# Modulation rows: three of eight weight tiles of the second half on VectorE instead of TensorE

## The chip, the core and the metric

The kernel runs on one core of one Trainium2 chip. The metric is the device time of one execution in microseconds (us). TensorE is called PE in the profile, VectorE DVE, ScalarE ACT, GpSimd POOL and SyncE SP; SP's queue issues nearly all the DMAs.

## What is computed

The reference is one layer of a diffusion backbone: 1024 latent tokens and 256 context tokens of width 1024, all in float32. What matters here is its beginning. Two vectors (the condition c and the learned vector of the context) go through silu and a 1024 x 6144 weight matrix; the first 2048 columns give the shift and the scale that modulate the normed tokens ahead of the first projection:

```python
mod = jax.nn.silu(c) @ w_mod[l] + b_mod[l]
mod_c = jax.nn.silu(c_ctx)[None, :] @ w_mod[l] + b_mod[l]
sh1, sc1, g1, sh2, sc2, g2 = jnp.split(mod, 6, axis=-1)
sh1c, sc1c, g1c, sh2c, sc2c, g2c = jnp.split(mod_c, 6, axis=-1)
h = modulate(rms_norm(x, norm1_w[l]), sh1, sc1)
hc = modulate(rms_norm(ctx, norm1_w[l]), sh1c, sc1c)
aq, ak, av, mq, mk, mv, mo, mg, ga, gm = split_in_proj(h @ w_in[l])
aqc, akc, avc, mqc, mkc, mvc, moc, mgc, gac, gmc = split_in_proj(hc @ w_in[l])
```

Behind it come windowed attention, a bidirectional mLSTM, a gated merge and a convolutional feed-forward part.

## The kernel before

`layer_kernel` runs the stages one after the other: `attention_setup` and `stage_startup` (the change is in the latter), then attention, mLSTM, the merges and the feed-forward tail. A matrix product of accuracy float32 is done with operands split into a high and a low part (`split_from`: ACT copies the high part, line 44; DVE subtracts it, line 49) and three matmuls (`mm3`, lines 90 to 92).

`stage_startup` works in this order:

- Lines 303 to 312: the small vectors are loaded and turned, and `sil` gets silu of both condition vectors: for each k one column pair, 128 x 2.
- Lines 373 to 380, the modulation rows: two halves i = 0 and 1, each with eight weight tiles of 128 x 1024 (512 KB, line 376). Each tile is the moving operand of two f32 matmuls, 512 columns each, with the 128 x 2 block `sil[:, k]` as weights; they accumulate in `pm[i]`, two rows for the two condition vectors. The tiles come from `block`, a ring of 11 buffers that is shared with the context tiles `x0` and `x1`, the later x tiles and the weights that follow. So a load waits until the tile 11 places ahead of it in the ring has been used.
- Lines 335 to 347, `modulation(i)`: the two rows are copied out of PSUM into `mrow` (half on DVE, half on ACT), turned by eight small transposes (`pmT`, line 341), and made into four columns of `mods` (bias and scale for latent and context tokens) by six DVE operations on 128 x 4.
- Lines 323 to 328, `norm`: squares and their sum on ACT (`xj`), the root on POOL, the scaling of the token tile on DVE (line 328).
- Lines 349 to 371: the normed context is turned on PE (`turn_context`, tiles `xct`), modulated and split on ACT and DVE (`hfc`, `hcH`, `hcL`). Blocks 0 and 1 need the first half of the modulation, blocks 2 and 3 the second.
- Lines 389 to 447: the weights for the context keys and values are loaded (line 70) and split, and the products `pkc` and `pvc` follow.
- Lines 396 to 407 and 448 to 468, `k_stack` and `context_keys`: the normed keys are doubled into the two tiles `kk` and `kl` of 128 x 512, turned, and stored.
- Lines 471 to 503: the context's mLSTM projections `cx`, with the turning and modulating of the latent tokens (`xt`, `hf`, `hH`, `hL`) between them.

PSUM: `bank` hands out eight banks by number; `tp_tile` takes banks 3, 4 and 5 in turn, `mm_tile` 0 and 1.

In this stage the order of instructions on each engine is set when the program is built, by a scheduler that goes by the order of the text, by dependencies and by its own model of times; on the chip each engine keeps to the order it was given. In attention the order on PE, DVE, ACT and POOL is pinned by hand (class `Pinned`; all pinned instructions show line 516).

The later modulation rows have another form already (`mod_product` and `mod_row`, lines 217 to 249): DVE multiplies each weight tile of 128 x 512 by the column of `sil` and adds (`macc`), and four matmuls with a 128 x 128 block of `macc` as weights and one column of `expo` (filled with -0.5) as the moving operand sum over the partitions; the factor -2 restores the sum.

Of the kernel before, what the change touches and what calls it, by code (L numbers as in the profile page):

```python
# [8 lines left out]
F32 = mybir.dt.float32  # L9
F32R = mybir.dt.float32r  # L10
AF = mybir.ActivationFunctionType
ALU = mybir.AluOpType
# [4 lines left out]
P = 128  # L17
D = 1024
# [3 lines left out]
KT = D // P  # L22
# [20 lines left out]
def copy_act(nc, out, in_, scale=1.0):  # L43
    nc.scalar.activation(out, in_, AF.Copy, scale=scale)  # L44
# [55 lines left out]
def layer_kernel(ctx: ExitStack, tc: tile.TileContext, A: dict, out: bass.AP, dbg=None):  # L100
# [71 lines left out]
    with ExitStack() as st:  # L172
        at = attention_setup(E, st)
        stage_startup(E, at)
        if "hT" in dbg:
            for k in range(KT):
                nc.sync.dma_start(dbg["hT"][0, k * P : (k + 1) * P], hH[k].bitcast(F32))
                nc.sync.dma_start(dbg["hT"][1, k * P : (k + 1) * P], hL[k].bitcast(F32))
        if dbg.get("stop") != "hT":
            stage_attention(E, st, at)  # L180
# [109 lines left out]

def stage_startup(E, at):
    nc, tc, A, ident, expo, vecT, mods = E.nc, E.tc, E.A, E.ident, E.expo, E.vecT, E.mods
    mm_tile, tp_tile, s_tile, wts = E.mm_tile, E.tp_tile, E.s_tile, E.wts
    H = KT // 2
    with ExitStack() as st:
        sp = st.enter_context(tc.tile_pool(name="st1", bufs=1, reuse_waits="tile"))
        wp = st.enter_context(tc.tile_pool(name="stw", bufs=2, reuse_waits="tile"))
        xp = st.enter_context(tc.tile_pool(name="stx", bufs=11, reuse_waits="tile"))

        def block(name):  # L300
            return xp.tile([P, D], F32, tag="x", name=name)
# [7 lines left out]
        sil = E.sil3  # L309
# [7 lines left out]
        def load(i):  # L317
            t = block(f"x{i}")
            src = A["ctx"][i * P : (i + 1) * P] if i < NCB else A["x"][(i - NCB) * P : (i - NCB + 1) * P]
            nc.sync.dma_start(t, src)  # L320
            return t

        def norm(i, t):
            junk = wp.tile([P, D], F32, tag="junk", name=f"xj{i}", bufs=1)
            nc.scalar.activation(junk, t, AF.Square, accum_out=ss[:, i : i + 1])
            nc.gpsimd.tensor_scalar(ss[:, i : i + 1], ss[:, i : i + 1], 1.0 / D, EPS, op0=ALU.mult, op1=ALU.add)
            nc.gpsimd.tensor_tensor(rs[:, i : i + 1], ss[:, i : i + 1], expo[:, 0:1], op=ALU.pow)
            nc.vector.tensor_scalar(t, t, rs[:, i : i + 1], None, op0=ALU.mult)
# [3 lines left out]
        pm = [[pm0[:2, 0:512], pm0[:2, 512:1024]], [mm_tile("pm2")[:2], mm_tile("pm3")[:2]]]  # L332
        bT = vecT[:, 32:48].rearrange("p (s k) -> p s k", s=2)

        def modulation(i):
            mrow = sp.tile([P, 1024], F32, name=f"mrow{i}", tag="mrow")[:2]
            nc.vector.tensor_copy(mrow[:, 0:512], pm[i][0])
            copy_act(nc, mrow[:, 512:1024], pm[i][1])
            pT = tp_tile(f"pmT{i}")
            for j in range(8):  # L340
                nc.tensor.transpose(pT[:, 2 * j : 2 * j + 2], mrow[:, j * P : (j + 1) * P], ident[:2, :2])
            pTv = pT[:, :16].rearrange("p (s k c) -> p s c k", s=2, c=2)
            ks = slice(H * i, H * i + H)
            for c in (1, 0):
                nc.vector.tensor_tensor(mods[:, 2 + c, ks], pTv[:, 0, c], bT[:, 0, ks], op=ALU.add)
                nc.vector.scalar_tensor_tensor(mods[:, c, ks], pTv[:, 1, c], 1.0, bT[:, 1, ks], op0=ALU.add, op1=ALU.add)
                nc.vector.tensor_tensor(mods[:, c, ks], mods[:, c, ks], vecT[:, 16 + H * i : 16 + H * i + H], op=ALU.mult)

        def modulated(c, k, hi, lo, src, nm):
            w = hi.shape[1]  # L350
            f = sp.tile([P, 512], F32, tag="hf", name=f"hf{nm}", bufs=3)[:, :w]
            nc.scalar.activation(f, src, AF.Identity, bias=mods[:, 2 + c, k : k + 1], scale=mods[:, c, k : k + 1])
            split_from(nc, hi, lo, f)
# [4 lines left out]
        def turn_context(k2):  # L358
            pt = tp_tile(f"xct{k2}")
            for j in range(2):  # L360
                for c in range(NCB):
                    k = 2 * k2 + j
                    nc.tensor.transpose(
                        pt[:, (2 * j + c) * P : (2 * j + c + 1) * P], xc[c][:, k * P : (k + 1) * P], ident
                    )
            return pt

        def context(k2, pt):
            for j in range(2):
                k = 2 * k2 + j  # L370
                modulated(1, k, *hc[k], pt[:, j * NCTX : (j + 1) * NCTX], f"c{k}")

        for i in range(2):
            for k in range(KT):
                w = block(f"wm{i}_{k}")
                nc.sync.dma_start(w, A["w_modA"][i][:, k])
                for n in range(2):
                    nc.tensor.matmul(
                        pm[i][n], sil[:, k], w[:, n * 512 : (n + 1) * 512], start=k == 0, stop=k == KT - 1
                    )  # L380
                if i == 0 and k in (3, 4):
                    xc.append(load(k - 3))
            if i == 0:
                modulation(0)
                for c in range(NCB):
                    norm(c, xc[c])
                for k2 in range(2):
                    context(k2, turn_context(k2))
        at.constants()
        wkc = wts.load(A["w_kc"], 256, block)  # L390
        pts = [turn_context(k2) for k2 in (2, 3)]
        modulation(1)
        for k2 in (2, 3):
            context(k2, pts[k2 - 2])

        def k_stack(kf, nh, name):
            w = nh * HD
            kk = wp.tile([P, 512], F32, tag="kk", name=f"kk{name}", bufs=1)
            kh = kk[:, : 2 * w].rearrange("p (h r d) -> p h r d", r=2, d=HD)
            kv = kf.rearrange("p (h d) -> p h d", d=HD)  # L400
            for r in range(2):
                copy_act(nc, kh[:, :, r].bitcast(F32R), kv)
            kl = wp.tile([P, 512], F32, tag="kl", name=f"kl{name}", bufs=1)
            kl4 = kl[:, : 2 * w].rearrange("p (h r d) -> p h r d", r=2, d=HD)
            for r in range(2):
                nc.vector.tensor_tensor(kl4[:, :, r].bitcast(F32R), kv, kh[:, :, r], op=ALU.subtract)
            return kk, kl
# [40 lines left out]
        def context_keys():  # L448
            for c in range(NCB):
                ps = pkc[c]  # L450
                sq = wp.tile([P, 256], F32, tag="sq", name=f"sqc{c}", bufs=1)
                nc.scalar.activation(sq, ps[:, :256], AF.Square)
                rstd = wp.tile([P, 4], F32, tag="ssc", name=f"ssc{c}", bufs=2)
                nc.vector.tensor_reduce(rstd, sq.rearrange("p (h d) -> p h d", d=HD), axis=AX.X, op=ALU.add)
                nc.gpsimd.tensor_scalar(rstd, rstd, 1.0 / HD, EPS, op0=ALU.mult, op1=ALU.add)
                nc.gpsimd.tensor_tensor(rstd, rstd, expo[:, :4], op=ALU.pow)
                kf = wp.tile([P, 256], F32, tag="qf", name=f"kcf{c}", bufs=2)
                kv4 = kf.rearrange("p (h d) -> p h d", d=HD)
                nc.vector.tensor_tensor(
                    kv4, ps[:, :256].rearrange("p (h d) -> p h d", d=HD), rstd[:, :, None].to_broadcast([P, NKV, HD]), op=ALU.mult  # L460
                )
                nc.vector.tensor_tensor(kv4, kv4, at.qw[:, 1, None, :].to_broadcast([P, NKV, HD]), op=ALU.mult)
                kk, kl = k_stack(kf, NKV, f"c{c}")
                for src, dst in ((kk, at.KcA), (kl, at.KcB)):
                    pt = tp_tile(f"kct{c}")
                    for h in range(NKV):
                        nc.tensor.transpose(pt[:, h * P : (h + 1) * P], src[:, h * P : (h + 1) * P], ident)
                    copy_act(nc, dst[:, :, c * P : (c + 1) * P], pt.rearrange("p (h t) -> p h t", h=NKV))
# [3 lines left out]
        for i in range(4):  # L472
# [5 lines left out]
            w = []  # L478
# [2082 lines left out]
```

## Time and profile before

| | |
|---|---|
| three runs, median | 1935.49 us |
| lowest and highest | 1934.72 and 1941.44 us |
| the profiled execution | 1934.33 us |
| its span, first to last instruction | 1932.5 us |
| its mean granted TensorE clock | 0.996 |
| DVE, ACT, POOL busy | 1348.9, 971.5, 344.5 us |
| HBM read and written | 201.67 and 74.00 MB |

A row of the timeline has start, length, engine, line, operation, output tile <- inputs, sizes and the count of like instructions; in brackets the idle time of the engine before it and what ended it. A group row has the count, the busy time and mean ns of one, and behind the bar the idle time before them. A row on a tile gives shortest, median and longest duration in ns. PEld is the weight load of PE, which overlaps the matmuls. Matmuls are pipelined, so the duration of one is longer than the step from one to the next. "issue" is time in which an engine waited for nothing that the profile shows. In the table by stage the clock is a share of full speed.

### The profile page before, as it was taken

To read this page: it belongs to the slowest core of one execution; us is meant where nothing else is said; L and a number is where in the kernel's file an instruction comes from. 1 tells how busy PE (TensorE), PEld (TensorE's weight loads), DVE (VectorE), ACT (ScalarE), POOL (GpSimd) and SP (SyncE) were. 2 spreads that over 40 slices of the span, in tenths; PEclk is the share of its full clock that TensorE was granted. 3 is DMA by queue.
4 is the path that set the end of the run, shared out by engine and by line. 5 is a ranking of instruction groups with operands and counts; after the bars stand their busy time and mean duration, and the time that the engine had idled before them with its cause. 6 is when DMAs were issued, how large, how long until landed. Compare 5 with 4: busy or idle time off the path is not lost.

```text
span 1932.5 us, 28336 instructions
## 1 busy us (share of the span) xinstructions
PE 1904.1 (99%) x10108; PEld 1648.8 (85%) x10108; DVE 1348.9 (70%) x2611; ACT 971.5 (50%) x1872; POOL 344.5 (18%) x594
## 2 busy tenths in 40 slices
PE   8999999999999999999999999999999999999999
PEld 3988888888888899999998788887888888888887
DVE  2877767767776456576676458359988888895564
ACT  4855556556556354646444323257545454464441
POOL 1323333333332132434231000010000000000000
PEclk9999999999999999999999999999999999999999
DMA  8733223223223321513145778312555544499741
GB/s 313 226 98 83 83 70 99 63 80 93 72 74 82 93 73 36 127 47 98 42 129 172 250 234 285 128 66 77 185 200 181 196 153 179 148 332 329 253 165 44
DMA packets 133246, 273.33 MB, mean 141 GB/s; under 512 B 14433, under 2 KB 46833, under 8 KB 129777
## 3 DMA queue, kind: packets, MB, share of 16 engines
q1 hardware_dynamic: 132336, 267.33, 41.8%
q0 software_dynamic: 768, 4.20, 1.4%
q8 instruction: 79, 1.29, 0.3%
q14 instruction: 63, 0.51, 0.1%
HBM read 201.67 MB, written 74.00 MB: 143 GB/s over the span
## 4 chain that ended last, share of the span: by engine, by line
PE 92%; DVE 4%; DMA 2%; ACT 1%; issue 1%; POOL 0%; SPq 0%; DVEq 0%; ACTq 0%; POOLq 0%
PE g L516 9%; PE kv L516 7%; PE pq L516 6%; PE mo L516 5%; PE op L516 5%; PE pa L2169 4%; PE pa L2167 4%; PE pa L2168 4%; PE s L516 4%; PE ya L516 4%; PE po L516 4%; PE pt L516 3%; PE ym L516 3%; PE q L516 2%; PE dx L2167 2%; PE dx L2168 2%
## 5 line engine op out<-in xcount | busy, mean ns | idle before, releaser
L516 DVE CUSTOM_DVE_ANT_0 P<-s,maskA,nsink 128x640 f32<-128x640 f32 (+1 forms) x112 | 103.4, 923 | 81.6 <-PE s L516 80.0
L516 ACT ACTIVATE P<-P,st 128x640 f32<-128x640 f32 (+1 forms) x128 | 102.4, 800 | 88.8 <-DVE st L516 88.7
L516 ACT ACTIVATE ph<-pt 128x512 fp32r<-128x512 f32 x152 | 90.3, 597 | 63.9 <-PE pt L516 62.3
L516 DVE TENSOR_TENSOR pl<-pt,ph 128x512 fp32r<-128x512 f32 x152 | 101.0, 680 | 25.9 <-ACT ph L516 25.7
L516 POOL TENSOR_SCALAR P<-P,st 128x640 f32<-128x640 f32 (+1 forms) x128 | 110.5, 881 | 32.0 <-ACT ph L516 10.9
L516 PE MATMUL g<-hH,fh 128*128 128x512 f32 x256 | 106.8, 417 | 0.2 <-ACT fo L516 0.2
L516 PE MATMUL g<-hH,fl 128*128 128x512 f32 x256 | 101.1, 395 | 0.0
L516 PE MATMUL g<-hL,fh 128*128 128x512 f32 x256 | 101.0, 395 | 0.0
L516 PE MATMUL pt<-ident,P 128*128 128x128 f32 x608 | 91.3, 273 | 3.8 <-DVE pl L516 3.8
L516 PEld LDWEIGHTS pt<-ident,P 128*128 128x128 f32 x608 | 75.7, 141 | 15.5 <-issue 3.9
L516 PE MATMUL pq<-w1h,hH 128*128 128x384 f32 (+1 forms) x256 | 87.1, 340 | 0.0
L516 PE MATMUL kv<-w1h,hH 128*128 128x384 f32 x256 | 86.9, 340 | 0.0
L516 PE MATMUL pq<-w1l,hH 128*128 128x384 f32 (+1 forms) x256 | 86.9, 340 | 0.0
L516 PE MATMUL pq<-w1h,hL 128*128 128x384 f32 (+1 forms) x256 | 86.5, 338 | 0.0
L516 PE MATMUL kv<-w1h,hL 128*128 128x384 f32 x256 | 86.1, 336 | 0.0
L516 PE MATMUL kv<-w1l,hH 128*128 128x384 f32 x256 | 86.1, 336 | 0.0
L516 PE MATMUL mo<-w1h,hH 128*128 128x256 f32 x256 | 72.5, 283 | 0.0
L516 POOL TENSOR_SCALAR ss<-ss 128x5 f32<-128x5 f32 x64 | 13.0, 204 | 332.3 <-DVE ss L516 329.3
L49 DVE TENSOR_TENSOR dfl<-drf,dfh 128x512 fp32r<-128x512 f32 x55 | 37.9, 691 | 48.6 <-ACT dfh L44 48.6
L516 PE MATMUL mo<-w1h,hL 128*128 128x256 f32 x256 | 71.8, 281 | 0.0
L516 PE MATMUL mo<-w1l,hH 128*128 128x256 f32 x256 | 71.7, 280 | 0.0
L44 ACT ACTIVATE dfh<-drf 128x512 fp32r<-128x512 f32 x55 | 34.4, 630 | 69.0 <-PE dy L2168 34.6
(620 smaller groups left out, 6338.3 us busy)
## 6 DMA issues: line engine op xcount, KB each, us to landing
ur<-in_w_up SPq DMA_DIRECT2D x22, 1024.0 KB, 5.3
wmb<-in_w_modB SPq DMA_DIRECT2D x64, 256.0 KB, 2.9
f_d<-cv SPq DMA_DIRECT2D x22, 512.0 KB, 2.9
wm<-in_w_modA SPq DMA_DIRECT2D x16, 512.0 KB, 8.8
fr<-in_w_g SPq DMA_DIRECT2D x32, 256.0 KB, 2.8
drf<-fs_d SPq DMA_DIRECT2D x15, 512.0 KB, 5.9
drw<-wt_d SPq DMA_DIRECT2D x14, 512.0 KB, 5.2
w1b<-in_w_cx SPq DMA_DIRECT2D x16, 388.0 KB, 4.8
```

Source lines behind the costliest of these rows:

```text
L44: nc.scalar.activation(out, in_, AF.Copy, scale=scale)
L49: (nc.vector if eng == "v" else nc.gpsimd).tensor_tensor(lo, src, hi.bitcast(F32), op=ALU.subtract)
L516: i = f(*a, **k)
L2167: nc.tensor.matmul(ps, lh, rh, start=start and i == 0, stop=False, skip_group_check=True)
L2168: nc.tensor.matmul(ps, lh, rl, start=False, stop=False, skip_group_check=True)
L2169: nc.tensor.matmul(ps, ll, rh, start=False, stop=stop and i == n - 1, skip_group_check=True)
```

## The change

In the second half (i = 1), the weight tiles k = 0, 2 and 4 are not multiplied on PE. DVE multiplies them, for each of the two condition vectors, by the column of `sil` and adds the products up in two tiles `side` of 128 x 1024. Behind the last weight tile, sixteen matmuls (eight blocks of 128 columns, two vectors) with a block of `side` as weights and one column of `expo` sum over the partitions into `side_sum`, a tile in PSUM bank 5, already in the turned form. `modulation(1)` multiplies these sums by -2 and adds them to the turned rows before the six operations on `mods`. The first of the two `side` tiles serves afterwards as `kk` and `kl`.

```diff
--- before.py
+++ after.py
@@ -290,7 +290,7 @@
 
 def stage_startup(E, at):
     nc, tc, A, ident, expo, vecT, mods = E.nc, E.tc, E.A, E.ident, E.expo, E.vecT, E.mods
-    mm_tile, tp_tile, s_tile, wts = E.mm_tile, E.tp_tile, E.s_tile, E.wts
+    bank, mm_tile, tp_tile, s_tile, wts = E.bank, E.mm_tile, E.tp_tile, E.s_tile, E.wts
     H = KT // 2
     with ExitStack() as st:
         sp = st.enter_context(tc.tile_pool(name="st1", bufs=1, reuse_waits="tile"))
@@ -339,7 +339,14 @@
             pT = tp_tile(f"pmT{i}")
             for j in range(8):
                 nc.tensor.transpose(pT[:, 2 * j : 2 * j + 2], mrow[:, j * P : (j + 1) * P], ident[:2, :2])
-            pTv = pT[:, :16].rearrange("p (s k c) -> p s c k", s=2, c=2)
+            pTv = pT[:, :16]
+            if i:
+                part_p = sp.tile([P, 16], F32, name="mpart")
+                both_p = sp.tile([P, 16], F32, name="mcol")
+                nc.vector.tensor_scalar(part_p, side_sum[:, :16], -2.0, None, op0=ALU.mult)
+                nc.vector.tensor_tensor(both_p, pTv, part_p, op=ALU.add)
+                pTv = both_p
+            pTv = pTv.rearrange("p (s k c) -> p s c k", s=2, c=2)
             ks = slice(H * i, H * i + H)
             for c in (1, 0):
                 nc.vector.tensor_tensor(mods[:, 2 + c, ks], pTv[:, 0, c], bT[:, 0, ks], op=ALU.add)
@@ -370,14 +377,32 @@
                 k = 2 * k2 + j
                 modulated(1, k, *hc[k], pt[:, j * NCTX : (j + 1) * NCTX], f"c{k}")
 
+        side = [sp.tile([P, D], F32, name=f"side{c}") for c in range(2)]
+        side_sum = bank(5, "side_sum")
+        ASIDE = ((), (0, 2, 4))
         for i in range(2):
             for k in range(KT):
                 w = block(f"wm{i}_{k}")
                 nc.sync.dma_start(w, A["w_modA"][i][:, k])
-                for n in range(2):
-                    nc.tensor.matmul(
-                        pm[i][n], sil[:, k], w[:, n * 512 : (n + 1) * 512], start=k == 0, stop=k == KT - 1
-                    )
+                if k in ASIDE[i]:
+                    for c in range(2):
+                        acc, f = side[c], sil[:, k, c : c + 1]
+                        if k == 0:
+                            nc.vector.tensor_scalar(acc, w, f, None, op0=ALU.mult)
+                        else:
+                            nc.vector.scalar_tensor_tensor(acc, w, f, acc, op0=ALU.mult, op1=ALU.add)
+                else:
+                    for n in range(2):
+                        nc.tensor.matmul(
+                            pm[i][n], sil[:, k], w[:, n * 512 : (n + 1) * 512], start=k == i, stop=k == KT - 1
+                        )
+                if i and k == 7:
+                    for j in range(8):
+                        for c in range(2):
+                            nc.tensor.matmul(
+                                side_sum[:, 2 * j + c : 2 * j + c + 1], side[c][:, j * P : (j + 1) * P], expo[:, 0:1],
+                                start=True, stop=True,
+                            )
                 if i == 0 and k in (3, 4):
                     xc.append(load(k - 3))
             if i == 0:
@@ -395,12 +420,12 @@
 
         def k_stack(kf, nh, name):
             w = nh * HD
-            kk = wp.tile([P, 512], F32, tag="kk", name=f"kk{name}", bufs=1)
+            kk = side[0][:, 0:512]
             kh = kk[:, : 2 * w].rearrange("p (h r d) -> p h r d", r=2, d=HD)
             kv = kf.rearrange("p (h d) -> p h d", d=HD)
             for r in range(2):
                 copy_act(nc, kh[:, :, r].bitcast(F32R), kv)
-            kl = wp.tile([P, 512], F32, tag="kl", name=f"kl{name}", bufs=1)
+            kl = side[0][:, 512:1024]
             kl4 = kl[:, : 2 * w].rearrange("p (h r d) -> p h r d", r=2, d=HD)
             for r in range(2):
                 nc.vector.tensor_tensor(kl4[:, :, r].bitcast(F32R), kv, kh[:, :, r], op=ALU.subtract)
```

## The prediction

> **What bounds the kernel now.** I read the page first, then the table by stage, then the chain that ended last, and then PE, DVE and the DMA queue in the stage that is edited.
>
> ```profile
> span 1932.5 us, 28336 instructions
> PE 1904.1 (99%) x10108; PEld 1648.8 (85%) x10108; DVE 1348.9 (70%) x2611; ACT 971.5 (50%) x1872; POOL 344.5 (18%) x594
> ```
>
> The whole kernel is TensorE work: 28.4 us of the span have no matmul in flight. Anything that takes work from PE and puts no wait in its place should show in the time. The question is how much, so the next view is the table by stage (length, busy time and instructions of each engine, granted clock, DMA share, GB/s).
>
> ```profile
> core 0: us, PE busy (x) PEld busy (x) DVE busy (x) ACT busy (x) POOL busy (x), PEclk, DMA share, GB/s
> 5.70:22.90 17.20, 17.20 (x49) 4.18 (x50) 2.19 (x3) 2.89 (x5) 1.49 (x4) 1.00 1.03 412
> 22.90:36.70 13.80, 13.80 (x33) 2.61 (x32) 4.29 (x14) 5.67 (x12) 0.00 (x0) 1.00 0.86 290
> 36.70:45.00 8.30, 8.16 (x68) 7.59 (x67) 4.47 (x14) 6.51 (x15) 1.48 (x4) 1.00 0.94 348
> 45.00:60.00 15.00, 12.49 (x78) 11.77 (x78) 11.65 (x20) 11.59 (x22) 5.02 (x8) 0.89 0.70 247
> 400.00:1000.00 600.00, 597.75 (x3827) 559.35 (x3826) 395.07 (x1024) 320.64 (x746) 196.19 (x371) 1.00 0.29 74
> ```
>
> The first modulation half (5.7 to 22.9 us) runs with the DMA engines full. The second (22.9 to 36.7), the one edited, is PE without a gap while DVE works 4.29 of 13.80 us. Far behind it PE is full as well (597.75 of 600 us), so a shift at the start is handed through to the end. The chain of waits says what happens between:
>
> ```profile
> 22.95 13.82 PE pm L378 x32
> ...
> 38.57 0.35 PE pmT L341 x4
> 39.46 1.02 ACT hfc L352 x2
> ...
> 42.62 1.05 ACT xj L325 x2
> ...
> 47.71 0.69 DVE w1l L49
> 48.44 0.39 PE pvc L91
> ```
>
> The 32 matmul instructions of the second half are on the chain; behind them the turned modulation row (pmT) frees ScalarE, and from 39.46 us the chain goes over ACT, POOL and DVE to the next weights at 48.44 us. So the edited stage is worth what it brings forward the moment at which mods are ready.
>
> **What is removed.** Three of eight weight tiles, two matmuls each, and every f32 matmul is two instructions here (16 matmuls show as 32).
>
> ```profile
> 22.88 13.89 PE L378 MATMUL pm<-wm,sil 128*2 128x512 f32 x32
> 36.71 1.09 PE L363 MATMUL xct<-ident,x 128*128 128x128 f32 x8
> ```
>
> From the first row's start to the next row's start lie 13.83 us, so one instruction takes 13.83 / 32 = 0.432 us. 3 tiles x 2 matmuls x 2 instructions = 12 go: **-5.19 us on PE**.
>
> **What is added on PE.** Sixteen matmuls with a 128x128 block of the VectorE sums as weights and one column of expo as the moving operand. The kernel has the same form already, for the rows ms of the later modulation:
>
> ```profile
> 159.52 1.09 PEld L516 LDWEIGHTS ms<-expo,macc 128*128 128x128 f32 x8
> 159.75 0.95 PE L516 MATMUL ms<-expo,macc 128*128 128x1 f32 x8
> L516 PEld LDWEIGHTS ms<-expo,macc x64: 187/192/196, 159.5 to 1187.1; 128*128 128x128 f32 x64
> L516 PE MATMUL ms<-expo,macc x64: 164/250/251, 159.8 to 1187.2; 128*128 128x1 f32 x64
> ```
>
> One row is four matmuls and shows eight records, so again two instructions each: 16 matmuls make 32. The step from one to the next is (0.95 - 0.25) / 7 = 0.10 us by the matmuls and (1.09 - 0.19) / 7 = 0.129 us by the weight loads. I take 0.115, between the two, since either may set the pace: 32 x 0.115 = **+3.7 us**, with ends at 3.2 and 4.1. So nearly three quarters of what is removed comes back: 128 columns of weights are loaded to move one column. Net on PE: **-1.5 us** (-1.1 to -2.0).
>
> Could the 3.7 us be hidden? In the text of the program they stand behind the last pm matmul, ahead of the transposes of the modulation row, and the row can only be finished with both. Between pm and pmT, PE now does eight xct transposes (the 1.09 us row above) while mrow is copied; the new matmuls join them in that place, and there is no PE gap there to fall into. So they count in full.
>
> **What is added on DVE.** Six operations on 128x1024: two plain multiplies (tile 0) and four multiply-adds (tiles 2 and 4); then a small multiply by -2 and a small add in the second modulation.
>
> ```profile
> L328 DVE TENSOR_SCALAR x<-x,rs 128x1024 f32<-128x1024 f32 x6 | 4.5, 752 | 11.8 <-POOL rs L327 11.8
> L516 DVE SCALAR_TENSOR_TENSOR macc<-wmb,sil,macc x56: 739/744/753, 109.0 to 1182.0; 128x512 f32<-128x512 f32 x56
> 29.18 1.36 DVE L49 TENSOR_TENSOR w1l<-w1b,w1h 128x512 fp32r<-128x512 f32 x2 [2.04 <-ACT w1h L44]
> 35.95 0.68 DVE L337 COPY mrow<-pm 2x512 f32<-2x512 f32 x1 [5.41 <-PE pm L378]
> 38.94 0.16 DVE L345 TENSOR_TENSOR mods<-pmT,vecT 128x4 f32<-128x4 f32 x1 [1.11 <-PE pmT L341]
> 14.17 0.33 SPq L376 DMA_DIRECT2D wm<-in_w_modA  x1
> wm<-in_w_modA SPq DMA_DIRECT2D x16, 512.0 KB, 8.8
> ```
>
> The multiply has its own form at 0.75 us. The multiply-add is known at 512 wide (0.744 us); at 1024 wide it lies between 1.0 (fixed share large) and 1.49 us (twice), and I take 1.25. Together 2 x 0.75 + 4 x 1.25 = 6.5 us (5.5 to 7.5). The cover: DVE is idle 13.80 - 4.29 = 9.5 us in the edited stage, 5.41 us of it in one piece ahead of the mrow copy. The last tile wanted, the fifth of its half, is issued at 14.17 us (the thirteenth wm load), and with the 8.8 us median to landing it is there near 23 us. Its two multiply-adds can then be done near 28 us even if the twelve small operations of the first modulation and of the context come first, while the five remaining tiles keep PE until 22.9 + 10 x 2 x 0.432 = 31.5 us. So the six operations cost nothing on the path. If that cover failed (a multiply-add standing ahead of the first mrow copy in DVE's order, for which pmT waits on PE), it would cost up to one such operation, 1.25 us; I take 0.
>
> The two small operations lie on the chain. The -2 can run while pmT is still turned; the add comes between pmT and mods. By the 0.16 us of the mods row each costs 0 to 0.16 us: 0 to 0.3, I take **+0.2 us**. PE does not wait for it at once: pkc begins with the four hc that the first modulation has made ready. Queued behind the add on DVE are the six mods operations and the hcL subtractions; ACT's hfc waits for them.
>
> **What is moved.** Weight tiles 0, 2 and 4 of the second half are released by DVE instead of PE, and PE passes the others sooner. The queue's next loads wait for just these releases:
>
> ```profile
> 24.79 2.04 SPq L70 DMA_DIRECT2D w1b<-in_w_kc  x2
> 29.94 2.05 SPq L320 DMA_DIRECT2D x<-in_x  x2
> 45.63 2.17 ACT L44 ACTIVATE w1h<-w1b 128x512 fp32r<-128x512 f32 x4
> ```
>
> Both are earlier or unchanged after the edit (the first x load waits for tile 3, which PE then reaches after one tile instead of three: 2 x 4 x 0.432 = 3.5 us), and the weights of the values were split at 45.63 us without a wait for their DMA, so the loads can follow a path that is 1 to 2 us earlier. I put this at 0. kk and kl, now halves of one side tile, keep their use one after the other: 0. The buffers of the stage shift in memory, and a later tile may wait for another old one; from the waits of PE in this stage, which are 0.3 to 1.8 us each (rows under the second rival), I bound that by -1 to +2 us and take 0, as no row shows such a wait now.
>
> **Sum:** -5.19 + 3.7 + 0.2 = -1.3 us. The profiled execution took 1934.33 us, 1.8 more than its span, and is 1.16 us under the median of the three runs (1935.49). 1934.33 - 1.3 = 1933.0 us, and on the scale of the median **1934.2 us**. About 0.5% (9.7 us) is what a measurement of this kernel can tell from no change, and no term of this sum reaches it.
>
> **The rivals.** First: *the gain is eaten behind the row*, time unchanged at 1935.5. It needs another limit between 38 and 48 us. For it: from 45 to 60 us PE is busy only 12.49 of 15 us, the waits there end with ACT, POOL and DVE work, and that order is fixed before the run. Against: this work starts from the mods in question, so it should move with them.
>
> Second: *a gain of the whole removal*. If the small matmuls fell into a wait of PE, or if the low clock behind the edited stage went away, it would be up to 5.2 - 0.2 = 5.0 us: 1930.5 us. The rows for the clock:
>
> ```profile
> 44.59 0.27 PE L420 MATMUL xt<-ident,x 128*128 128x128 f32 x1
> 45.41 0.55 PE L420 MATMUL xt<-ident,x 128*128 128x128 f32 x3 [0.54 <-DVE x L328]
> 46.30 0.38 PE L90 MATMUL pvc<-w1h,hcH 128*128 128x256 f32 x1 [0.34 <-ACT w1h L44]
> 48.44 0.39 PE L91 MATMUL pvc<-w1l,hcH 128*128 128x256 f32 x1 [1.76 <-DVE w1l L49]
> 51.00:52.00 1.00, 1.00 (x6) 1.00 (x6) 1.00 (x2) 0.18 (x1) 0.00 (x0) 0.50 1.11 395
> 53.00:54.00 1.00, 1.00 (x11) 1.00 (x10) 0.67 (x2) 0.73 (x1) 0.00 (x0) 1.00 0.87 328
> ```
>
> From 44.59 to 48.44 us PE has four transposes and one matmul, and soon after it runs at half clock: six matmuls in a microsecond where it later does eleven. The second of those rows has the clock back; over some 3.4 us the stage loses about 1.7 us.
>
> Third: *the new matmuls bring such a low clock themselves*. For some 3.7 us PE then moves single columns, with the 1.09 us of xct transposes behind them; if the chip takes that for idleness, pkc runs at half clock for 3.4 us. The price is up to 1.7 us, and less where pkc's end is not what is waited for: -1.3 + 1.7 = +0.4, 1935.9 us. Against it: PE is never without an instruction there, and the ms rows, 0.95 us each, are too short to say.
> [...]
>
> Fourth, and on the other side: *a wait for a PSUM bank*. side_sum is asked for ahead of the loop in bank 5, and the context transposes take banks 3, 4, 5 in turn, the first block bank 5. Now these transposes run early:
>
> ```profile
> 15.79 0.44 PE L363 MATMUL xct<-ident,x 128*128 128x128 f32 x2
> ```
>
> If the bank is given in the order of asking, the first block can be turned only after the second modulation has read side_sum. Its two pieces (hfc and hcH; four pieces fill ACT from 39.46 to 42.62 us, so two take 1.6 us) then stand in the ACT chain behind the mods instead of before them, and pkc, which begins with them, leaves PE empty and may bring the low clock: -1.3 + 1.6 + 1.7 = +2.0 us, 1937.5 us. It decides as soon as these transposes stand behind the second modulation's row in PE's order. Against it: if a bank is given to whoever is ready first, they run near 16 us as now.
>
> That the change does not do what it says, the tiles still multiplied on PE, is excluded by the diff: the two branches exclude each other.
>
> **How the numbers follow.** Forecast (0.5 to 3 us gained) 0.45; eaten 0.2; whole removal 0.1; low clock 0.1; bank 0.15. The predicted time is the forecast's, 1934.2 us. Its own range is 1932.5 to 1935.0. With the rivals the cases reach from 1930.5 to 1937.5; the edges take in the DVE cover (+1.25) and the memory shift (+2) on the dear side, and the three runs alone, from 1934.72 to 1941.44, say that a median can lie some us high: **1930.5 to 1939.0**. No case reaches 9.7 us to either side. What is left for over 0.5% is something in the order of the later stages that none of these cases holds: faster 0.02, same 0.95, slower 0.03.
>
> **What would show it.** Right: 20 instead of 32 pm matmuls in the second half, 32 new ones on side_sum at 0.10 to 0.13 us, six DVE operations done before pm ends, the second mods at 37 to 38 us instead of 38.94, and the value product pvc over 1 us earlier. Wrong: a PE wait on the side tiles, new matmuls at over 0.16 us each, the first xct transposes behind 35 us, a half clock between 32 and 42 us, or mods early and pvc not. A time under 1930 or over 1940 us would make the sum itself wrong.

## The result and the profile after

| | before | after |
|---|---|---|
| median | 1937.03 us | 1940.93 us |
| lowest to highest | 1932.38 to 1941.52 us | 1936.97 to 1951.98 us |
| ratio (95% interval) | 1 | 1.0019 (1.0011 to 1.0028) |
| the profiled execution | 1934.33 us | 1940.86 us |
| its mean granted clock | 0.996 | 0.992 |

Each side has 22 runs. The changed kernel is 3.9 us slower, with an interval that leaves out 1. That is under the 0.5% of the prediction, so by that bound it is "the same", though 22 runs a side tell 0.1 to 0.3% from nothing. It is on the other side of the forecast (1.3 us faster) and its time lies above the range, which reached to 1939.0 us. Of the 6.7 us between 1934.2 us and 1940.93 us, 1.5 us are the median of before itself: 1937.03 us here, 1935.49 us in the three runs that the prediction started from. The two profiled executions differ by 6.5 us and overstate it: the one of before was 2.7 us under its median here, the one of after at its median.

The first line of the page of the changed kernel already says what kind of time came:

```profile
span 1939.1 us, 28390 instructions
PE 1910.5 (99%) x10128; PEld 1657.8 (85%) x10128; DVE 1355.6 (70%) x2619; ACT 969.8 (50%) x1872; POOL 344.1 (18%) x594
```

PE is idle 28.6 us, as before (28.4). Of the 6.6 us of span, 6.4 us are more **PE busy** time. Yet the change took 12 instructions of 0.432 us from PE and gave it 32 small ones that last 3.7 us together, so at an equal clock PE should be busy 1.5 us less. Busy time that grows while work shrinks means slower work, and the granted clock is the column to read next. The table by stage of the changed kernel, second modulation half and what follows it:

```profile
23.36:36.38 13.02, 13.02 (x59) 5.60 (x57) 7.63 (x15) 6.14 (x13) 0.00 (x0) 1.00 0.98 353
36.38:46.60 10.22, 10.22 (x61) 9.66 (x60) 5.27 (x17) 4.62 (x12) 0.74 (x2) 0.67 0.69 227
```

The edited stage is shorter, 13.02 us against 13.80, and four context transposes (0.58 us) now stand inside it: without them it is 12.4 us, 1.4 us less than before, much as the prediction's net for PE (-1.5). The stage behind it, the key products, had a clock of 1.00 over 8.30 us before; now it has 0.67 over 10.22 us. The timeline of PE in this place shows it instruction by instruction:

```profile
23.36 1.88 PE L396 MATMUL pm<-wm,sil 128*2 128x512 f32 x4
25.17 0.66 PE L370 MATMUL xct<-ident,x 128*128 128x128 f32 x4
25.75 7.03 PE L396 MATMUL pm<-wm,sil 128*2 128x512 f32 x16
32.71 3.73 PE L402 MATMUL side_sum<-expo,side 128*128 128x1 f32 x32
36.38 0.41 PE L341 MATMUL pmT<-ident,mrow 2*128 2x2 f32 x4
37.09 1.05 PE L370 MATMUL xct<-ident,x 128*128 128x128 f32 x4
38.08 0.58 PE L341 MATMUL pmT<-ident,mrow 2*128 2x2 f32 x4
43.24 0.41 PE L91 MATMUL pkc<-w1l,hcH 128*128 128x256 f32 x1
44.92 0.28 PE L92 MATMUL pkc<-w1h,hcL 128*128 128x256 f32 x1
50.92 0.58 PE L91 MATMUL pvc<-w1l,hcH 128*128 128x256 f32 x1
```

The 20 pm instructions and the 32 small ones are as forecast. Right behind the small ones everything takes longer: four transposes 1.05 us instead of the 0.66 of the second row, a key product 0.41 us at 43.24 us and 0.28 at 44.92. The second row of values (pvc) comes at 50.92 us, 2.5 us later than before instead of 1 us earlier; 0.5 us of that is there already at the first pm row of this half (23.36 us against 22.88). Two stretches of one microsecond from the table by stage mark the edges of the low clock, and two more the next one:

```profile
36.00:37.00 1.00, 1.00 (x9) 0.97 (x10) 0.52 (x2) 0.00 (x0) 0.00 (x0) 0.86 0.99 393
43.00:44.00 1.00, 1.00 (x9) 1.00 (x8) 0.24 (x2) 1.00 (x4) 0.00 (x0) 0.72 0.88 336
50.00:51.00 1.00, 0.68 (x4) 0.56 (x4) 1.00 (x3) 1.00 (x3) 0.92 (x2) 0.69 0.00 0
53.00:54.00 1.00, 1.00 (x7) 1.00 (x7) 1.00 (x3) 0.33 (x1) 0.67 (x1) 0.61 0.77 198
```

The clock is 0.50 in each microsecond from 37 to 43 us. A share of 0.86 in the first row is then half clock from 36.7 us on, 0.72 in the second half clock up to 43.6: some 6.8 us, twice the length of the stretch that the prediction read behind pvc in the profile of before. That stretch is still there, a little later (50.4 to 53.8).

The clock is not all. The timeline of DVE in the changed kernel, and behind it two rows of before:

```profile
28.42 2.48 DVE L393 SCALAR_TENSOR_TENSOR side<-wm,sil,side 128x1024 f32<-128x1024 f32 x2
36.48 0.17 DVE L346 TENSOR_SCALAR mpart<-side_sum 128x16 f32<-128x16 f32 x1 [3.84 <-PE side_sum L402]
36.57 0.68 DVE L49 TENSOR_TENSOR w1l<-w1b,w1h 128x512 fp32r<-128x512 f32 x1
38.70 0.17 DVE L347 TENSOR_TENSOR mcol<-pmT,mpart 128x16 f32<-128x16 f32 x1 [1.44 <-PE pmT L341]
38.79 1.28 DVE L49 TENSOR_TENSOR w1l<-w1b,w1h 128x512 fp32r<-128x512 f32 x2
39.99 0.15 DVE L352 TENSOR_TENSOR mods<-mcol,vecT 128x4 f32<-128x4 f32 x1
40.21 0.69 DVE L49 TENSOR_TENSOR w1l<-w1b,w1h 128x512 fp32r<-128x512 f32 x1
41.07 0.16 DVE L354 TENSOR_TENSOR mods<-mods,vecT 128x4 f32<-128x4 f32 x1
```

```profile
36.56 1.27 DVE L49 TENSOR_TENSOR w1l<-w1b,w1h 128x512 fp32r<-128x512 f32 x2
39.48 0.16 DVE L347 TENSOR_TENSOR mods<-mods,vecT 128x4 f32<-128x4 f32 x1
```

The side tiles are done at 30.9 us, ahead of need. But the multiplication by -2 stands in DVE's order ahead of the subtractions for the key weights (w1l), waits 3.84 us for side_sum, and they wait behind it. Afterwards three of them stand between the add and the last of the mods. In the kernel before, two of them ran at 36.56 us while DVE waited for the turned row, and none stood behind it. The mods end at 41.23 us, before at 39.64; counted from the first pm row of the half that is 17.87 us against 16.76, 1.1 us later. Ahead of pvc the order has changed too: a scaling of an x tile (0.75 us, at 49.51 us) and three transposes that wait for it stand there, where before DVE split the value weights at once. From the start of the normed keys to pvc it is 1.92 us (49.00 to 50.92), before 1.07 (47.37 to 48.44): some 0.8 us more.

### The profile page after: what moved, and what is told of

It is laid out like the page before. It is cut to its first block, busy times and chain, and to the rows that moved or that the text cites. A ratio compares the mean times of both kernels' runs of the same rounds, so it can differ in the third digit from the quotient of the medians.

```text
span 1939.1 us, 28390 instructions
## 1 busy us (share of the span) xinstructions
PE 1910.5 (99%) x10128; PEld 1657.8 (85%) x10128; DVE 1355.6 (70%) x2619; ACT 969.8 (50%) x1872; POOL 344.1 (18%) x594
## 4 chain that ended last, share of the span: by engine, by line
PE 91%; DVE 4%; DMA 3%; issue 1%; ACT 1%; POOL 0%; SPq 0%; DVEq 0%; ACTq 0%; POOLq 0%
PE g L541 9%; PE kv L541 7%; PE pq L541 7%; PE op L541 5%; PE ym L541 5%; PE mo L541 4%; PE pa L2194 4%; PE pa L2192 4%; PE pa L2193 4%; PE s L541 4%; PE po L541 3%; PE pt L541 3%; PE ya L541 3%; PE q L541 2%; PE dx L2194 2%; PE dx L2193 2%
## 5 line engine op out<-in xcount | busy, mean ns | idle before, releaser
L2192 PE MATMUL dx<-dwh,dfh 128*128 128x512 f32 x176 | 68.5, 389 | 0.0
```

The source lines that it names most:

```text
L2192: nc.tensor.matmul(ps, lh, rh, start=start and i == 0, stop=False, skip_group_check=True)
```

## The experiments

The main theory, after this reading: the single-column matmuls bring the low clock over pkc (third rival of the prediction), and it costs more than was allowed for. Against it: the added order on DVE and in bank 5, which makes the second mods late, or the shift in memory, which makes a weight load of a later row late. All ratios are to the kernel before, in runs beside each other on one chip, with 95% intervals.

**Single columns or wide ones, added to the kernel before.** The two kernels add some 3.6 us of PE work at the same place, behind the last pm matmul, with nobody waiting for the result: the first in the form of the change, the second as four matmuls of 512 columns.

```diff
+                if i and k == 7:
+                    extra = E.fl_tile("extra")
+                    for j in range(16):
+                        o = j % 8 * P
+                        nc.tensor.matmul(extra[:, j : j + 1], w[:, o : o + P], expo[:, 0:1], start=True, stop=True)
```

```diff
+                if i and k == 7:
+                    extra = E.fl_tile("extra")[:2]
+                    for j in range(4):
+                        o = j % 2 * 512
+                        nc.tensor.matmul(extra, sil[:, k], w[:, o : o + 512], start=True, stop=True)
```

> The kernel before, with sixteen single-column matmuls added behind the second half of the rows (weights from the last weight tile, results in an unused bank and not used). Nothing is taken off PE, no DVE work, wait or memory is added. Clock theory: +3.7 us on PE and then half clock over pkc for 3.4 or 6.8 us, so that the time is 3.7 to 7 us over before. Order theory and memory theory: the small matmuls cost only their 3.7 us, clock unchanged near 42 us, time at most 3.7 us over before.

> The kernel before with four wide matmuls (eight instructions of 512 columns, 3.46 us) added in the place where the run with single columns had sixteen small ones; results not used. Clock theory: PE takes 3.5 us longer, the clock over pkc stays whole, and the time is 2.5 to 4 us over before, against 8.5 us (ratio 1.0044) with single columns. If the low clock came from the longer stage, from the transposes or from the copies behind it, half clock over pkc and 6 to 8 us over before.

Measured: single columns 1945.67 us, ratio 1.0044 (1.0028 to 1.0059); wide 1939.93 us, ratio 1.0013 (1.0003 to 1.0022). The added work and what follows it in the table by stage, single columns first, then wide:

```profile
38.11:41.70 3.59, 3.59 (x33) 3.59 (x33) 1.12 (x2) 1.63 (x3) 0.74 (x2) 1.00 0.90 290
41.70:52.00 10.30, 10.30 (x66) 9.95 (x66) 3.69 (x12) 4.42 (x11) 0.74 (x2) 0.67 0.52 177
```

```profile
36.29:39.82 3.53, 3.53 (x9) 0.60 (x8) 1.98 (x4) 3.26 (x6) 1.17 (x3) 1.00 0.93 310
39.82:50.00 10.18, 10.18 (x89) 10.00 (x89) 7.14 (x17) 8.51 (x18) 2.19 (x6) 1.00 0.79 261
```

The work itself is as long, 3.59 and 3.53 us. Behind the single columns PE gets 66 instructions through in 10.3 us at a clock of 0.67, behind the wide ones 89 in 10.2 us at 1.00. In these two kernels, then, it is the form of the matmul, not its time, that brings the low clock. Nor is it the many weight loads by themselves: PEld is as full behind the wide ones (10.00 of 10.18 us) at a clock of 1.00.

What the low clock costs is best read against before, whose order on DVE the kernel with single columns keeps:

```profile
55.68 0.58 PE L91 MATMUL pvc<-w1l,hcH 128*128 128x256 f32 x1 [1.53 <-DVE w1l L49]
47.30 0.28 PE L91 MATMUL pvc<-w1l,hcH 128*128 128x256 f32 x1
```

The first row is the kernel with single columns: pvc comes 31.40 us after the first pm row of the half (24.28 us), against 25.56 before, 5.84 us later, of which the added matmuls are 3.7. So some 2.1 us are the price at this place, and by the ratio the whole execution is 8.5 us longer (5.4 to 11.4) for 3.7 us of work, more than the 7 us that the clock theory had at most. One minus the mean granted clock, times the time, is the time lost to a low clock: 12.0 us in these runs and 7.8 in those of before beside them.

The second row is the kernel with wide ones, and the two must not be compared in price. The scheduler gave it another order on DVE: the value weights are split from 45.76 us on, ahead of the normed keys, so pvc follows pkc without a wait and no low clock comes there (1.00 up to 50.00 us; 6.6 us lost in its runs, 9.2 in before beside them). So the 0.0031 between the two ratios, some 6 us, holds more than the form of the matmuls.

**Single columns in three groups.** The changed kernel with tiles 0, 1 and 2 on DVE instead of 0, 2 and 4, and the small matmuls spread behind tiles 5, 6 and 7, so that no group is longer than 1.6 us.

```diff
-        ASIDE = ((), (0, 2, 4))
+        ASIDE = ((), (0, 1, 2))
...
-                if i and k == 7:
-                    for j in range(8):
+                if i and k > 4:
+                    for j in ((0, 1, 2), (3, 4, 5), (6, 7))[k - 5]:
```

> The changed kernel with tiles 0, 1 and 2 aside instead of 0, 2 and 4, and the sixteen small matmuls spread behind the last three weight tiles, six, six and four between the wide ones. [...] Memory theory: the wait at 105 us stays, as the memory is that of the changed kernel.

Measured: 1942.59 us, ratio 1.0031 (1.0021 to 1.0042). PE, and the table by stage behind the last group:

```profile
30.72 1.58 PE L402 MATMUL side_sum<-expo,side 128*128 128x1 f32 x12
32.23 1.88 PE L396 MATMUL pm<-wm,sil 128*2 128x512 f32 x4
34.04 1.50 PE L402 MATMUL side_sum<-expo,side 128*128 128x1 f32 x12
35.47 1.88 PE L396 MATMUL pm<-wm,sil 128*2 128x512 f32 x4
37.27 1.05 PE L402 MATMUL side_sum<-expo,side 128*128 128x1 f32 x8
50.80 0.39 PE L91 MATMUL pvc<-w1l,hcH 128*128 128x256 f32 x1 [2.38 <-DVE w1l L49]
```

```profile
38.26:46.40 8.14, 7.91 (x64) 7.23 (x63) 4.87 (x16) 6.38 (x16) 1.82 (x4) 1.00 0.81 268
```

The same 32 instructions with wide matmuls between them bring no low clock (1.00 over the 8.14 us behind the last group), and the clock of the runs is nearly back (9.5 us lost, against 7.8 before on this chip and 12.8 in the changed kernel). The time does not come back: pvc is as late as in the changed kernel (50.80 us, though this execution is 0.8 us later already at the end of the first half), now behind a wait of 2.38 us for the split of its weights on DVE, with PE idle instead of slow, and the mods end at 41.90 us. So the low clock over pkc is not the only thing that holds this stage. The order on DVE, which still has subtractions between the add and the mods, is the likely other one; this run does not separate it.

**The order on DVE.** The changed kernel, with the multiplication by -2 put behind all subtractions of the key weights.

```diff
+                first = nc.vector.tensor_scalar(part_p, side_sum[:, :16], -2.0, None, op0=ALU.mult)
+                for s in wts.subs:
+                    dep = mybir.DependencyInfo(mybir.DependencyClass.NoSync, mybir.DependencyReason.DATA)
+                    tc.add_manual_dep(first.ins, s.ins.name, dep, reason="order")
```

> The changed kernel with one thing ordered by hand: on DVE the multiply by -2, which waits for the last small matmul, stands behind the four subtractions of the key weights instead of ahead of them (PE's order then also has the transposes that want bank 5 behind the second mods row). Order theory: the second mods end 1.3 to 2 us earlier than after the change when measured from the start of the second half (17.9 us there, 16 to 16.6 here), and the part of the time that is not lost to a low clock falls by 1 to 1.5 us. Clock theory: the half clock behind the small matmuls stays, so the time stays over that of before (ratio 1.000 to 1.002). Memory theory: macc still waits ahead of V.

Measured: 1942.13 us, ratio 1.0019 (1.0008 to 1.0031), the same as the changed kernel. On DVE the edit did what it should; this is its timeline, and what the trace says of the context transposes between 30 and 46 us:

```profile
36.36 0.17 DVE L346 TENSOR_SCALAR mpart<-side_sum 128x16 f32<-128x16 f32 x1 [0.63 <-PE side_sum L405]
37.65 0.17 DVE L350 TENSOR_TENSOR mcol<-pmT,mpart 128x16 f32<-128x16 f32 x1 [1.11 <-PE pmT L341]
38.15 0.28 DVE L357 TENSOR_TENSOR mods<-mods,vecT 128x4 f32<-128x4 f32 x2
```

```profile
L373 PE MATMUL xct<-ident,x x4: 411/418/421, 42.6 to 43.2; 128*128 128x128 f32 x4
  PE xct L373: 3.7, 1
```

The mods end at 38.43 us, 2.8 us earlier than in the changed kernel. Yet the last four context transposes, which were at 37.09 us there, now stand behind most of pkc, at 42.6 us, and ScalarE waits 3.7 us for them. These four need PSUM bank 5, which side_sum held until DVE read it; in the kernel before they ran with the other four ahead of the modulation row. So the experiment took one wait away and let another in, and pkc ran at a low clock as in the changed kernel (0.67 from 36.25 to 46.70 us). It does not tell what the order on DVE alone is worth. The kernel with this order and the memory of before, further down, has the same flaw: its last four transposes stand at 43.2 us and ScalarE waits 3.5 us for them.

**The shift in memory.** In the changed kernel the first weight load of the later modulation rows (wmb) is issued at 103.07 us instead of 84.85, and DVE waits for it ahead of the first V block. That comes with the new layout of the memory, in which its buffer probably overlaps one of the x tiles of the first stage:

```profile
106.46 0.49 DVE L541 TENSOR_SCALAR macc<-wmb,sil 128x512 f32<-128x512 f32 x1 [1.10 <-DMA wmb<-in_w_modB]
106.86 0.22 DVE L541 TENSOR_TENSOR V<-pq,V 128x64 fp32r<-128x64 f32 x1
```

Two kernels separate it: the kernel before with the memory of the changed one (the side tiles there only hold kk and kl), and the changed kernel with its side tiles in memory that is free at that time (the rotation tables, joined into one tile T4 for this), kk and kl back in their own. A third has the order of the last experiment and this memory together.

```diff
+        side = [sp.tile([P, D], F32, name=f"side{c}") for c in range(2)]
+        room = sp.tile([P, 32], F32, name="room")
...
-            kk = wp.tile([P, 512], F32, tag="kk", name=f"kk{name}", bufs=1)
+            kk = side[0][:, 0:512]
```

> The kernel before, with nothing moved off PE: only its memory is laid out as after the change (two side tiles and a small one in the first pool, kk and kl in the first side tile), so that the ring of x tiles reaches over the places of wmb and macc of the attention stage. Memory theory: the first wmb load is issued near 103 us instead of 84.85, macc stands directly ahead of V on DVE and waits for it about 1 us, the first attention qt is 1.3 to 2 us later than before, and the time is 1 to 3 us longer (ratio 1.0005 to 1.0015). Clock theory and order theory: no row up to 95 us changes, no half clock near 37 us, and the time is that of before.

```diff
-        side = [sp.tile([P, D], F32, name=f"side{c}") for c in range(2)]
+        side = [at.T4[:, 2 * c : 2 * c + 2].rearrange("p i b d -> p (i b d)") for c in range(2)]
```

> The changed kernel with its side tiles placed in the rotary tables' room, which is not yet in use, and kk and kl back in their own tiles: the later pools keep their places. Memory theory: the first wmb load is issued before 95 us, macc waits for nothing, and of the 3.0 us that the changed kernel is late at 110 us, 1.5 to 2 are gone. Clock theory: side_sum still takes 3.7 us and pkc behind it still runs at half clock for 3.4 or 6.8 us. Order theory: the second mods still end 1 to 1.6 us later than in the kernel before.

> The changed kernel with the order of the run before and with its side tiles in the rotary tables' room, so that the later pools keep their places; the single-column matmuls stay. Order and memory theory together: what is not lost to a low clock is 1 to 2.5 us under that of before, as the sum of the prediction had it (-1.3). Clock theory: the mean granted clock stays 0.001 to 0.0025 under that of before (2 to 5 us), so that the time is not under before by more than 1 us (ratio 0.9995 to 1.002).

Measured: memory alone 1936.53 us, ratio 1.0 (0.9989 to 1.001), with the load at 101.52 us; the change without the shift 1937.70 us, 1.0008 (0.9999 to 1.0018); order and memory together 1940.54 us, 1.0013 (1.0 to 1.0026). By itself the late load costs nothing that can be measured, where the memory theory had 1 to 3 us. The order and the memory together were to bring the part that is not lost to a low clock 1 to 2.5 us under before; it is 1.4 us above (1929.6 against 1928.2 us), with the transposes late as said. In the changed kernel taking it away may be worth up to 2 us, but the intervals overlap and the two profiles do not differ by the load alone. PE in the kernel without the shift:

```profile
33.27 3.73 PE L403 MATMUL side_sum<-expo,T 128*128 128x1 f32 x32
37.49 0.65 PE L371 MATMUL xct<-ident,x 128*128 128x128 f32 x4
38.07 0.58 PE L342 MATMUL pmT<-ident,mrow 2*128 2x2 f32 x4
```

The small matmuls begin 0.6 us later in this execution, and the low clock begins only behind the transposes and lasts about 3.4 us instead of 6.8 (the clock is 0.50 at 38 us, 0.84 between 41 and 42, full afterwards). The same instructions meet the low clock at different points; part of the spread between runs may come from that, which was not shown.

**The sum by wide matmuls.** The same three tiles on DVE, but summed by four matmuls of 512 columns that add into the row's own banks, with a column of ones (pick, 128 x 2 for each vector) as weights: no side_sum, no bank 5, no multiplication and no add on DVE. Once with the memory of the kernel before, run twice, and once with that of the changed kernel.

```diff
-                            nc.tensor.matmul(
-                                side_sum[:, 2 * j + c : 2 * j + c + 1], side[c][:, j * P : (j + 1) * P], expo[:, 0:1],
-                                start=True, stop=True,
-                            )
+                            nc.tensor.matmul(
+                                pm[1][n], pick[:, 2 * c : 2 * c + 2], side[c][:, n * 512 : (n + 1) * 512], start=False, stop=c == 1
+                            )
```

> The changed kernel with another way to sum over the partitions: four wide matmuls (8 instructions of 512 columns, 3.46 us) with a 128 x 2 block of ones and zeros as weights add the side tiles straight into the rows pm; no side_sum, no bank 5, no multiply by -2, no add, the side tiles in the rotary tables' room. Clock theory: no half clock at 36 us. With order and memory also out of the way: PE -5.19 + 3.46 = -1.7 us, second mods 1.5 to 2 us earlier than before from the start of the half, time 1 to 3 us under before (ratio 0.9985 to 0.9995). If the three causes are not all: 1.000 or more.

> The kernel of e3_wide_sum once more, so that its first figure (0.999, from 0.9979 to 1.0001) gets a second one on another set of runs. Clock theory (the single columns bring the half clock, and their 3.7 us were all of the cost): the four wide matmuls are eight instructions of 0.432 us, 3.5 us, so the PE work is 1.7 us shorter than before and there is no half clock near 40 us: 1.5 to 3 us under the kernel before, ratio 0.998 to 0.9993. Rival, that any edit of this stage only reshuffles the dips of the clock and the first figure was chance: ratio 0.9995 to 1.001.

> The wide sum with the memory of the changed kernel: side in the stage's own pool, kk and kl in it, so that the first weight load of the later modulation rows is issued some 17 us later again. If the shift in memory costs nothing that counts, as its run alone said (ratio 1.0): the same time as the wide sum with the old memory within 1 us, ratio 0.998 to 0.9995. If the shift costs the 1.1 us that the multiply-add was seen to wait ahead of the first V block, or takes a dip of the clock with it: 1 to 3 us more than the other run of this pair, ratio 0.999 to 1.001.

Measured: 1934.44 us, ratio 0.999 (0.9979 to 1.0001); again 1933.31 us, 0.9984 (0.9975 to 0.9993); with the memory of the changed kernel 1933.26 us, 0.9986 (0.9976 to 0.9996). The last two ran beside each other and are 2.6 us under the 1935.89 us of before. PE of the second run, one row of its DVE, and the table by stage behind the sum:

```profile
23.72 1.88 PE L393 MATMUL pm<-wm,sil 128*2 128x512 f32 x4
25.53 1.09 PE L364 MATMUL xct<-ident,x 128*128 128x128 f32 x8
26.55 7.03 PE L393 MATMUL pm<-wm,sil 128*2 128x512 f32 x16
33.42 3.60 PE L399 MATMUL pm<-T,pick 128*2 128x512 f32 x8
45.68 0.39 PE L91 MATMUL pvc<-w1l,hcH 128*128 128x256 f32 x1
```

```profile
44.94 0.68 DVE L49 TENSOR_TENSOR w1l<-w1b,w1h 128x512 fp32r<-128x512 f32 x1
```

```profile
37.02:45.68 8.66, 8.00 (x64) 7.16 (x64) 4.80 (x15) 8.17 (x19) 1.81 (x5) 1.00 0.43 165
45.68:60.00 14.32, 13.93 (x94) 13.21 (x95) 13.03 (x24) 12.77 (x24) 4.81 (x7) 1.00 0.67 234
```

The sum takes 3.60 us, no less than the small matmuls did. But the eight context transposes are together again ahead of it, the clock stays at 1.00 over pkc and over pvc as well, and pvc comes 21.96 us after the second half's first pm (45.68 - 23.72), against 25.56 before and 27.56 in the changed kernel. This version beats both kernels. But the 3.6 us at pvc are more than the 1.7 us of PE work that it saves (12 instructions of 0.432 us less, 8 more): the scheduler also put the first split of the value weights ahead of the keys on DVE (the 44.94 us row), where before it stood behind them at 47.71 us and PE waited 1.76 us for it. That is so in all three runs. So the gain is that of the whole kernel; how much of it is the removal and how much the other order on DVE, no run separates. The rival, that any edit here only reshuffles the low clock, has the second and third run against it; the first alone did not exclude 1.

## Why the prediction was wrong

**What bounds the kernel** was read rightly: PE, with a shift at the start handed through. Of the 6.6 us of the profiled span, 6.4 are PE time.

**Removed on PE**: right, 20 instructions are left of 32.

**Added on PE**: 3.7 us forecast. The 32 matmuls start between 32.7 and 36.2 us, 3.7 us with the last one. The row of ms, four matmuls long, was enough to price them.

**Added on DVE**: the multiply-add was put at 1.25 us for 128x1024 and took 1.28 (28.42 us row: two in 2.48). The cover held: done at 30.9 us, with PE on pm until 32.7.

**The two small operations** were put at 0.2 us, by their duration. This step failed. Each takes 0.17 us, but DVE works in order (the subtractions behind the multiplication sat out its 3.84 us), and what counts is where they stand. The prediction named what is queued behind the add, and did not ask what is queued behind the multiplication, which waits for PE: the key-weight subtractions, which used to fill DVE's wait for the turned row. The mods came 1.1 us later, counted from the first pm row of the half (1.6 us by the clock of the profile, 41.23 against 39.64), where the forecast had them 1 to 2 us earlier.

**Memory shift**, taken at 0 within -1 to +2: the load that comes 18 us later was not foreseen, since no wait for it existed before, but 0 is what the single test (ratio 1.0) and the pair with the wide sum (0.9984 and 0.9986) show.

**Third rival, the low clock.** This is the step that weighs most. It had a chance of 0.1 and a price of up to 1.7 us; the sum of the likeliest case took no low clock at all, a term put at nothing. "PE is never without an instruction there" was the reason against it, and it is no reason: from 36.38 to 46.60 us PE was busy 10.22 of 10.22 us and the clock was 0.67. And the price assumed one stretch of 3.4 us; the profile has 6.8 us at half clock, 3.4 us lost, in that place, and a further stretch near 112 us (0.50 from 112 to 115 us), where before had none (1.00 from 109 to 115 us). In these runs 3.7 us of single columns in one piece brought the low clock (0.67 behind them) and pieces of 1.05 to 1.58 us did not (1.00); what length is enough, none of them tells. That it is the single columns is shown by the two added forms, 0.67 behind 3.59 us of them and 1.00 behind 3.53 us of wide ones. That the chip takes them for idleness, the condition that the prediction gave this rival, no run shows.

By the means of the runs: one minus the granted clock, times the time, is 12.8 us in the 22 runs of the changed kernel and 8.6 us in the 84 runs of before beside the experiments, 4.2 us more. The remainder, time at full clock so to say, is 1928.8 and 1928.2 us, 0.6 us more where the forecast had 1.3 less: 1.9 us that the clock does not explain. The order on DVE, ahead of the mods and ahead of pvc, bank 5 and the shift in memory are the candidates. In the changed kernel without the shift the remainder is 1927.7 us, 0.8 under before on its chip. In the wide sum it is 1925.9 to 1926.8, which is 1.4 to 2.0 us under before on the same chips; the work saved on PE is 1.7, but the other order on DVE is in this figure too. These means are over different chips and each is uncertain by half a microsecond to one; the split is an estimate from them. And where the single columns were spread out the clock came nearly back and the time did not, so the low clock is the larger part by this count, not the whole.

**Fourth rival, bank 5.** False as it was put: the first context transposes still run at 16.27 us. But the bank did matter: the last four transposes waited for it and stood ahead of the second part of the turned row.

**First rival, the gain eaten behind the row**: there in part, by DVE's order: the larger delay sits ahead of the mods (36.5 to 41.2 us), where the prediction looked for it in the work that starts from them, and the x tile of 49.51 us is a smaller one in that work.

**What stays open**: how the 1.9 us divide between the order on DVE, bank 5 and the shift in memory (0 to 2 us inside the changed kernel), since the test of the order moved the transposes; what the wide sum would gain with the order that DVE had before; and why the profile of the changed kernel has more stretches of low clock hundreds of microseconds on.

## What to carry to other kernels

Count on PE not only the time of the matmuls but how many columns they move: here 3.7 us of single-column matmuls in one piece slowed the wide ones behind them (clock 0.67 over 10.22 us), pieces of up to 1.6 us did not (1.00 over 8.14 us), so sum with a column of ones as weights and the wide tile moving. An operation of 0.2 us that waits on another engine can cost the wait of everything queued behind it, here 3.84 us of DVE; look for what used to fill that wait. When PE's busy time grows while its work shrinks (here 1904.1 to 1910.5 us, at 0.996 and 0.992), read the granted clock first. And when an edit changes the program, compare the order of the engines behind it before a difference is put down to the edit: here the scheduler moved the split of the value weights ahead of the keys in the kernels with wide matmuls added, and nothing in those edits asks for it.

## What was not expected of the hardware

- 32 f32 instructions that move one column against 128 columns of weights took 3.6 to 3.7 us without a gap, and within about a microsecond the clock was 0.50 (in the changed kernel they ended near 36.4 us, and it was 0.50 from 37 us on); 8 instructions of 512 columns took 3.5 to 3.6 us at the same place and left it at 1.00.
- The low clock lasted some 6.8 us behind the single columns in one piece in three kernels, by the share over the stretch behind them: the changed kernel (0.67 over 10.22 us; they began at 32.71 us), the kernel with them added (0.67 over 10.30 us) and the changed kernel with another order on DVE (0.67 over 10.45 us). In the kernel without the shift, where they began at 33.27 us, it lasted some 3.4 us (0.84 over 10.60 us).
- Moving three eighths of a row of weights to DVE does not need the sums turned: a sum over partitions into the row's own PSUM banks costs PE as much (3.60 us) as the turned one (3.73 us) and takes no bank and no DVE operation.
